# Hybrid encoder trunk: which tiles stand in a layer's opening, and where block 0's squares are summed

## The chip, the cores and the metric

The kernel runs on one core of a Trainium2 chip. The metric is device time in microseconds (us) of one execution; lower is better. The core has five engines with a queue each: TensorE (PE, matmuls, with its weight loads shown as PEld), VectorE (DVE), ScalarE (ACT), GpSimd (POOL) and SyncE (SP, which issues transfers). ACT issues transfers too; they are then named ACTq. Engines wait for each other by semaphores, and each engine works through its own instructions in order.

## The reference, cut to what matters

Two layers of an encoder over 2048 tokens of width 1024, float32. Each layer normalises the input, projects it by one wide matrix, and feeds the parts to a gated delta scan (branch A) and to a Conformer convolution (branch B):

```python
for l in range(2):
    h = rms_norm(x, norm_w[l])                        # mean of squares over 1024 channels
    proj = h @ w_in[l]                                # q,k,v | z_a | a,b | cf_val, cf_glu | z_b | gates
    q, k, v = silu(depthwise_conv(qkv, 5 taps))       # 4 heads of 128
    g, beta = f(a), sigmoid(b)                        # 16 scalar columns per token
    o = delta_forward(q, k, v, g, beta) + delta_backward(...)
    y_a = (rms_norm(o) * silu(z_a)) @ w_dn_out        # gate path of branch A
    u = silu(layer_norm(depthwise_conv(cf_val * sigmoid(cf_glu), 31 taps)))
    y_b = (u * silu(z_b)) @ w_cf_out                  # gate path of branch B
    x = x + (gate_a * y_a + gate_b * y_b) @ w_out
return rms_norm(x, final_norm_w)
```

## The kernel before, in words

Data lie channel-major: 8 tiles of 128 channels (`KD = 8`, index k) by 2048 tokens, the tokens in four blocks of 512 (`NB`). A normalised block `h` is kept as two parts, a high one and a low one (`split`, L156: ACT writes the high part by L157, DVE the low part by L158). Each weight tile of 128 columns (`weight`, L160) is loaded by SP as `wraw` in two pieces and split likewise into `whi` and `wlo`. A dense tile takes, for each k, three 128x512 matmuls: `whi` with `xhi` (L174), `whi` with `xlo` (L175), `wlo` with `xhi` (L176). One column tile on one block is thus 24 matmuls.

A layer runs through these stages: the opening (norm and first column tiles, block by block), four heads (convolved q, k and v tiles, the Conformer tile, then two gate-path tiles, `act_tile`, with columns 24 + j into `zb` and 12 + j into `za`), the first half of the merge-gate tiles (`gates(0)`), the delta scan, and the merge.

**The opening of layer 0.** The generator `first_norm` (L287) normalises the four blocks, and the code that makes column tiles pulls it on by `need` and `step_lead`. For a block: x is loaded by SP in 8 tiles, ACT squares them (L308), the squares are added up, ones times the sum (`token_sum`, four 128x1 matmuls, L200) gives the sum over channels for each token, DVE makes the reciprocal root (from `nv`, L316, to `nr`), `spread` (L206, L208) puts it on all partitions, DVE multiplies x by it (L327), and `split` makes `h`. Block 0 adds its squares on DVE, blocks 1 to 3 on POOL (L310). Block 3 loads its x twice: once into the buffers of the squares, since the tiles for x are still in use, and later for the product.

On TensorE a block of the opening has 64 matmuls: 16 of the scalar tile (`scalar_tiles`, L398; high and low part of the 16 scalar columns stand in one weight tile `wab`; L408, L409) and 24 each of the k and q tiles of head 0 (columns 4 and 0). The scalar tile's sum is copied out by ACT to `ab` (L411) and transposed by TensorE (L414) into one PSUM tile for all blocks. The k and q sums go to `cin` (L529); after each half of the tokens DVE convolves them (L553).

**Buffers.** The staging pool `st` has three buffers of 128x512 for the whole kernel: squares (`sqa`, `sq`), the diagonal matrices of `spread` (`dg`), `ab`, the gate-path outputs (`ao`) and others. Dense sums take three PSUM tiles (`pd`), the rest five (`pz`).

**What sets the order.** Instructions are given to the engines in the order of a schedule that is made when the program is built, from the written order and from the buffers; the excerpts below show it. Beside this there is a planner by hand: `post` and `back` hold generators of pieces of later work (keys, values, Conformer norms), and each `dense` pumps them on by a credit (`rate`, in us per tile: 3.0, 3.7 and 4.5 for convolved tiles, others of the heads, and gates). After `gates(0)`, filler steps run while `back` isn't empty (`while self.back` in `layer`). The filler is `gates(1)` and then `early_merge`, whose matmuls read `uop`. The delta scan (`delta`) pulls the rest of the filler between its own steps by a written plan. At its end, the last chunk's output is squared on ACT (L1022), scaled (L1040), transposed (L1045), multiplied by the gate path (L1046), stored and read back as `gop`, whose matmuls begin the merge.

## Time and profile before

| What | Value |
|---|---|
| median of 3 runs (range) | 3219.36 us (3217.04 to 3219.66) |
| the profiled execution | 3223.96 us, its span 3222.2 us |
| granted TensorE clock, mean of the span | 0.987 |
| TensorE busy | 3101.0 us (96%) |
| VectorE, ScalarE, GpSimd busy | 2401.9 us (75%), 1393.5 us (43%), 302.2 us (9%) |
| opening of layer 0: first dense matmul, first matmul of block 3 | 22.26 us, 96.26 us |

In the rows of the timeline there stand the start in us from the span's start, the duration in us, the engine, the line, the operation, output<-input, the count, and in brackets how long the engine had been idle and what released it. A row of waits reads: engine, its tile and line, what it waited for, the total in us, how often, the longest. A dense matmul's duration (0.38 us at the full clock) is longer than its share of the engine, since matmuls overlap: starts are 0.21 to 0.22 us apart, at half clock 0.42 to 0.43. A 128x1 sum of four columns shows as eight matmuls.

### The profile page before, as it was taken

How to read it: one execution, taken by the hardware profiler on the slowest of the kernel's cores; microseconds unless marked ns; L12 is line 12 of the kernel's file. 1: busy time of each engine (PE TensorE's matmuls, PEld its weight loads, DVE VectorE, ACT ScalarE, POOL GpSimd, SP SyncE). 2: the span in 40 equal slices, each digit the busy share in tenths (PEclk: the TensorE clock that was granted, in tenths of full speed). 3: DMA queues.
4: the chain of work that ended last, by engine and by line, in shares of the span. 5: the costliest groups of instructions: out<-in, count | busy, mean ns of one | idle time of the engine just before them, and what ended most of it. 6: DMA issues, size and time to landing. Idle time of an engine off the chain costs nothing. (4 is left out here: it accounts for less than half of the span.)

```text
span 3222.2 us, 51090 instructions
## 1 busy us (share of the span) xinstructions
PE 3101.0 (96%) x19110; PEld 2711.5 (84%) x19110; DVE 2401.9 (75%) x4409; ACT 1393.5 (43%) x3104; POOL 302.2 (9%) x297
## 2 busy tenths in 40 slices
PE   6999999999999999799999999999999999989997
PEld 5788888888889998687888888888888999877786
DVE  7789898987555687645666989898955567867655
ACT  5625252522344466533345242425234445655332
POOL 3000000000022231000000000000002122200000
PEclk9999999999999999899999999999999999999999
DMA  4233232334687785654413131314358777856644
GB/s 139 88 96 94 84 100 78 102 108 132 215 289 231 261 270 174 191 187 128 141 50 107 66 116 62 119 59 122 116 188 269 236 254 246 265 155 208 206 128 147
DMA packets 427030, 501.67 MB, mean 156 GB/s; under 512 B 95712, under 2 KB 260192, under 8 KB 426784
## 3 DMA queue, kind: packets, MB, share of 16 engines
q1 hardware_dynamic: 354032, 388.58, 38.9%
q10 hardware_dynamic: 64688, 80.09, 7.1%
q0 software_dynamic: 8064, 29.76, 2.4%
q8 instruction: 150, 2.46, 0.3%
q14 instruction: 96, 0.79, 0.1%
HBM read 342.74 MB, written 155.58 MB: 155 GB/s over the span
## 5 line engine op out<-in xcount | busy, mean ns | idle before, releaser
L174 PE MATMUL pd<-h,whi 128*128 128x512 f32 x2816 | 1091.7, 388 | 0.0
L176 PE MATMUL pd<-h,wlo 128*128 128x512 f32 x2816 | 1071.3, 380 | 2.3 <-DVE wlo L158 2.3
L175 PE MATMUL pd<-h,whi 128*128 128x512 f32 x2816 | 1072.1, 381 | 0.0
L728 DVE SCALAR_TENSOR_TENSOR cacc<-gp,vec,cacc 128x1009 f32<-128x1009 f32 (+1 forms) x480 | 615.5, 1282 | 37.8 <-ACT cacc L726 34.7
L174 PEld LDWEIGHTS pd<-h,whi 128*128 128x128 f32 x2816 | 534.6, 190 | 79.3 <-issue 1.4
L176 PEld LDWEIGHTS pd<-h,wlo 128*128 128x128 f32 x2816 | 534.4, 190 | 79.5 <-DVE wlo L158 3.9
L175 PEld LDWEIGHTS pd<-h,whi 128*128 128x128 f32 x2816 | 534.5, 190 | 72.9 <-issue 1.9
L157 ACT ACTIVATE whi<-wraw 128x512 fp32r<-128x512 f32 x400 | 243.0, 624 | 488.6 <-PE pd L175 346.6
L158 DVE TENSOR_TENSOR wlo<-wraw,whi 128x512 fp32r<-128x512 f32 x400 | 279.7, 713 | 175.8 <-ACT whi L157 163.9
L553 DVE SCALAR_TENSOR_TENSOR acc<-cin,vec,acc 128x1022 f32<-128x1022 f32 (+1 forms) x192 | 246.9, 1300 | 14.7 <-ACT acc L551 13.6
L176 PE MATMUL pd<-yhi,wlo 128*128 128x512 f32 x512 | 195.3, 381 | 8.0 <-DVE wlo L158 7.9
L174 PE MATMUL pd<-yhi,whi 128*128 128x512 f32 x512 | 194.7, 380 | 1.4 <-ACT whi L157 1.3
L175 PE MATMUL pd<-ylo,whi 128*128 128x512 f32 x512 | 194.0, 379 | 0.0
L808 ACT ACTIVATE go<-pd,vec 128x512 f32<-128x512 f32 x128 | 87.0, 680 | 133.2 <-PE pd L176 122.6
L529 ACT ACTIVATE cin<-pd 128x512 f32<-128x512 f32 x96 | 57.0, 593 | 156.3 <-PE pd L176 156.1
L174 PE MATMUL pd<-gop,whi 128*128 128x512 f32 x256 | 99.9, 392 | 20.5 <-ACT gop L157 19.3
L176 PEld LDWEIGHTS pd<-yhi,wlo 128*128 128x128 f32 x512 | 96.7, 189 | 25.6 <-DVE wlo L158 12.2
L174 PE MATMUL pd<-uop,whi 128*128 128x512 f32 x256 | 102.9, 402 | 12.8 <-ACT uop L157 7.1
L1210 ACT ACTIVATE gt<-gt 128x1024 f32<-128x1024 f32 x64 | 67.6, 1058 | 108.1 <-DMA gt<-gt 98.9
L740 ACT ACTIVATE ao<-pd 128x512 f32<-128x512 f32 x64 | 38.3, 598 | 170.0 <-PE pd L176 169.9
L976 ACT ACTIVATE dm<-pz,eg 128x128 f32<-128x128 f32 x240 | 68.5, 368 | 98.8 <-PE pz L970 93.7
L174 PEld LDWEIGHTS pd<-yhi,whi 128*128 128x128 f32 x512 | 96.8, 189 | 16.4 <-ACT whi L157 3.0
(296 smaller groups left out, 4837.0 us busy)
## 6 DMA issues: line engine op xcount, KB each, us to landing
wraw<-w_in SPq DMA_DIRECT2D x240, 256.0 KB, 3.2
gt<-go ACTq DMA_DIRECT2D x128, 256.0 KB, 3.4
dl<-gr SPq DMA_DIRECT2D x128, 256.0 KB, 5.1
dl<-kq SPq DMA_DIRECT2D x64, 512.0 KB, 5.9
dl<-kv SPq DMA_DIRECT2D x64, 512.0 KB, 5.2
gt<-gt SPq DMA_DIRECT2D x64, 512.0 KB, 5.0
wraw<-w_out SPq DMA_DIRECT2D x96, 256.0 KB, 3.0
kq<-acc SPq DMA_DIRECT2D x16, 1024.0 KB, 5.5
```

The costliest lines, as they stand in the source:

```text
L157: self.nc.scalar.activation(hi, src, AF.Copy)
L158: self.nc.vector.tensor_tensor(out=lo, in0=src, in1=hi.bitcast(F32), op=ALU.subtract)
L174: mm(ps, whi[:, k, :], xhi, start=k == 0, stop=False)
L175: mm(ps, whi[:, k, :], xlo, start=False, stop=False)
L176: mm(ps, wlo[:, k, :], xhi, start=False, stop=k == kk - 1)
L529: nc.scalar.activation(cut(t[:, o + b * NB:o + (b + 1) * NB]), sort(ps), AF.Copy)
L553: self.nc.vector.scalar_tensor_tensor(out=out, in0=t[:, k:k + n], scalar=wc(k), in1=out, op0=ALU.mult, op1=ALU.add)
L728: self.nc.vector.scalar_tensor_tensor(out=acc, in0=t[:, k:k + n], scalar=wc(k), in1=acc, op0=ALU.mult, op1=ALU.add)
L740: nc.scalar.activation(cut(o), sort(ps), func)
L808: nc.scalar.activation(cut(o), sort(ps), AF.Identity, bias=self.vec[:, V_GB + j:V_GB + j + 1])
L976: nc.scalar.activation(hv(o1)[:, hd, :], pq[:, hd, :], AF.Copy, scale=eg[:, hd:hd + 1])
L1210: nc.scalar.activation(gt, gt, AF.Sigmoid)
```

## The change

The opening of each layer takes other tiles. `opening` runs, for each block, the scalar tile and the two gate-path tiles of head 0 (`zb` column 24 and `za` column 12) k by k: two scalar matmuls, three of `zb`, three of `za`, then the next k; in block 3 they run one tile after the other. The transposes of a block's scalar tile (`turned`) are written at k = 3 of the next block. The convolved k and q tiles of head 0 follow after the opening over all four blocks, as those of the other heads do. The gate paths of heads 1 to 3 are made after the Conformer tiles of the head ahead of them; after the last head no gate path follows. The sum of gate paths, convolved tiles and scalar tiles is the same as before. The gate tiles of head 0 no longer pump the planner's credit. Block 0's squares aren't added on DVE: for each k four 128x1 matmuls (`token_add`, L205 in the changed file) add the square into the same four PSUM columns. The lines of the changed file are shifted: L308 is L314 there, L408/L409 are L422/L423, L411 is L445, L414 is L429, L208 is L213, the opening's gate outputs are written by L449, L1022 is L1046, L1040 is L1064, L1045 is L1069, L1163 is L1187.

```diff
--- before.py
+++ after.py
@@ -199,6 +199,11 @@
         for i in range(n):
             self.nc.tensor.matmul(ps[:, i:i + 1], src[:, i * P:(i + 1) * P], self.ones[:, 0:1],
                                   start=True, stop=True)
+
+    def token_add(self, ps, src, n, first, last):
+        for i in range(n):
+            self.nc.tensor.matmul(ps[:, i:i + 1], src[:, i * P:(i + 1) * P], self.ones[:, 0:1],
+                                  start=first and i == 0, stop=last, skip_group_check=True)
 
     def spread(self, ps, r, n):
         dg = self.pst.tile([P, NB], F32, tag="st", name="dg").rearrange("p (a b) -> p a b", b=P)
@@ -299,18 +304,21 @@
             if blk < 3:
                 for k in range(KD):
                     self.load(x[k], src[k])
-            acc = self.st("sqa")
-            eng = nc.gpsimd if blk else nc.vector
+            acc = None if blk == 0 else self.st("sqa")
+            ps = self.pz()
+            eng = nc.gpsimd
             for k in range(KD):
-                sq = self.st("sq0") if k else acc
+                sq = self.st("sq0") if k or not blk else acc
                 if blk == 3:
                     self.load(sq, src[k])
                 nc.scalar.activation(sq, sq if blk == 3 else x[k], AF.Square)
-                if k:
+                if not blk:
+                    self.token_add(ps, sq, 4, k == 0, k == KD - 1)
+                elif k:
                     eng.tensor_tensor(out=acc, in0=acc, in1=sq, op=ALU.add)
             yield
-            ps = self.pz()
-            self.token_sum(ps, acc, 4)
+            if blk:
+                self.token_sum(ps, acc, 4)
             v = self.sm(4, "nv")
             r = self.sm(4, "nr")
             nc.vector.tensor_scalar(out=v, in0=ps[:, 0:4], scalar1=1.0 / D, scalar2=EPS,
@@ -361,11 +369,13 @@
         self.gt_d = self.drm.tile([16, P, L], F32, name=f"gt{l}")
         self.o_d = self.drm.tile([NCH, P, H, P], F32, name=f"o{l}")
         self.og_d = self.drm.tile([H, P, L], F32, name=f"og{l}")
+        pt = self.opening()
         for j in range(H):
-            self.head(j)
+            self.head(j, pt)
             self.conformer(j)
-            self.act_tile(24 + j, self.zb_d[j], AF.Silu)
-            self.act_tile(12 + j, self.za_d[j], AF.Silu)
+            if j + 1 < H:
+                for col, dst in self.gate_paths(j + 1):
+                    self.act_tile(col, dst, AF.Silu)
         for blk in range(4):
             self.back.append(self.conformer_norm(blk))
         self.rate = R3
@@ -395,25 +405,51 @@
         nc.scalar.activation(w[:, :, 32:128], self.ones[:, None, 0:96].to_broadcast([P, KD, 96]), AF.Copy, scale=0.0)
         self.wab = w
 
-    def scalar_tiles(self):
+    def gate_paths(self, j):
+        return (24 + j, self.zb_d[j]), (12 + j, self.za_d[j])
+
+    def opening(self):
         nc = self.nc
-        w = self.wab
+        mm = nc.tensor.matmul
         pt = self.pz()
-
-        def block(blk):
-            xs = self.hx(blk)
-            ps = self.pd()
+        cols = self.gate_paths(0)
+        ws = [self.weight(self.a["w_in"][self.l, c], KD) for c, _ in cols]
+        turn = deque()
+
+        def scalar_steps(ps, xs):
             for k in range(KD):
                 xhi, xlo = (mix(x) for x in xs(k))
-                nc.tensor.matmul(ps, w[:, k, :], xhi, start=k == 0, stop=False)
-                nc.tensor.matmul(ps, w[:, k, :], xlo, start=False, stop=k == KD - 1)
-            ab = self.st("ab")
-            nc.scalar.activation(cut(ab[0:32, :]), sort(ps[0:32, :]), AF.Copy)
+                mm(ps, self.wab[:, k, :], xhi, start=k == 0, stop=False)
+                mm(ps, self.wab[:, k, :], xlo, start=False, stop=k == KD - 1)
+                yield
+
+        def turned(blk, ab):
             for i in range(4):
                 c = 4 * blk + i
                 nc.tensor.transpose(pt[:, c * 32:(c + 1) * 32], ab[0:32, i * P:(i + 1) * P], self.ident[0:32, 0:32])
 
-        return block, pt
+        for blk in range(4):
+            self.need(blk)
+            xs = self.hx(blk)
+            pss = [self.pd() for _ in range(3)]
+            runs = [scalar_steps(pss[0], xs)] + [self.dense_steps(ps, w, xs, KD) for ps, w in zip(pss[1:], ws)]
+            for group in [runs] if blk < 3 else [[r] for r in runs]:
+                for k in range(KD):
+                    for r in group:
+                        next(r)
+                    if k == 3 and turn:
+                        turned(*turn.popleft())
+                    if k % (2 if blk < 3 else 4) == 0:
+                        self.step_lead(2 if k == 0 else 1)
+            ab = self.st("ab")
+            nc.scalar.activation(cut(ab[0:32, :]), sort(pss[0][0:32, :]), AF.Copy)
+            turn.append((blk, ab))
+            for ps, (_, dst) in zip(pss[1:], cols):
+                o = self.st("ao")
+                nc.scalar.activation(cut(o), sort(ps), AF.Silu)
+                self.astore(dst[:, blk * NB:(blk + 1) * NB], o)
+        turned(*turn.popleft())
+        return pt
 
     def scalars(self, pt):
         nc, l, a = self.nc, self.l, self.a
@@ -503,7 +539,7 @@
         nc.vector.tensor_copy(t[:, 0:2 * pad], prev[:, HALF - pad:HALF + pad])
         return t, 2 * pad
 
-    def conv_tiles(self, cols, block=None):
+    def conv_tiles(self, cols):
         nc = self.nc
         self.rate = R1
         ws = [self.weight(self.a["w_in"][self.l, c], KD) for c in cols]
@@ -515,20 +551,13 @@
                 cur.append(self.padded(half, TAPS, prev[i], "cin") if half or not i else None)
             for b in range(2):
                 blk = 2 * half + b
-                self.need(blk)
-                if block:
-                    self.step_lead(2)
-                    block(blk)
                 for i, c in enumerate(cols):
-                    self.step_lead(2)
                     ps = self.pd()
                     self.dense(ps, ws[i], self.hx(blk), KD)
                     if cur[i] is None:
                         cur[i] = self.padded(half, TAPS, prev[i], "cin")
                     t, o = cur[i]
                     nc.scalar.activation(cut(t[:, o + b * NB:o + (b + 1) * NB]), sort(ps), AF.Copy)
-            if half == 0 and self.l:
-                self.need(2)
             for i, c in enumerate(cols):
                 t, o = cur[i]
                 prev[i] = t
@@ -563,15 +592,10 @@
             if q % 2:
                 yield
 
-    def head(self, hd):
-        nc = self.nc
-        v_ = nc.vector
+    def head(self, hd, pt):
         if hd == 0:
-            block, pt = self.scalar_tiles()
-            kt, qt = self.conv_tiles([4, 0], block)
             self.post.append(self.scalars(pt))
-        else:
-            kt, qt = self.conv_tiles([4 + hd, hd])
+        kt, qt = self.conv_tiles([4 + hd, hd])
         vs = self.pds.tile([P, 16], F32, tag="vs", bufs=2, name="vs")
         self.post.append(self.keys(hd, kt, qt, vs))
         vt, = self.conv_tiles([8 + hd])
```

Where the instructions stand now, at three places. ACT, from the end of block 0 of layer 0's opening: `ab` is the scalar tile's copy, `ao` are the gate outputs, `sqa` and `sq0` block 2's squares, `h1` is block 1. Before:

```order
L411 ACTIVATE ab_301<-pd_284 32x512
L529 ACTIVATE cin_174<-pd_329 128x512
L308 ACTIVATE sqa_407<-x0m_396 128x512
L308 ACTIVATE sq0_409<-x0m_396 128x512
L308 ACTIVATE sq0_412<-x0m_396 128x512
L308 ACTIVATE sq0_415<-x0m_396 128x512
L157 ACTIVATE h1_231<-x0_106 128x512 x2
L308 ACTIVATE sq0_418<-x0h_397 128x512
```

and of the change:

```order
L445 ACTIVATE ab_398<-pd_250 32x512
L157 ACTIVATE h1_261<-x0_106 128x512
L449 ACT_TABLE_LOAD
L449 ACTIVATE ao_400<-pd_251 128x512
L449 ACTIVATE ao_403<-pd_252 128x512
L151 DMA zb0_173<-ao_400 128x512
L157 ACTIVATE h1_261<-x0_106 128x512
L151 DMA za0_172<-ao_403 128x512
L157 ACTIVATE h1_261<-x0_106 128x512 x2
L314 ACTIVATE sqa_435<-x0m_424 128x512
L157 ACTIVATE h1_261<-x0_106 128x512
L314 ACTIVATE sq0_438<-x0m_424 128x512
```

Two evictions to staging buffers and their stores now stand ahead of block 2's squares. `sqa_435` is given the buffer of `ao_400` and `sq0_438` that of `ao_403`; `sq0_441` and all later squares of the block are given the buffer of `sq0_438`, as the third one belongs to `ab_398`.

TensorE, at the end of block 1: L200 is the sum of block 2's squares, L213 its spread, L429 the transposes of blocks 0 and 1. Before, the sum of block 2 stands in the middle of block 1 (`L408`, `L174` to `L176` with `h1`):

```order
L176 MATMUL pd_496<-h1_231,wlo_155 128x512
L200 MATMUL pz_430<-con_90,sqa_407 128x1 x4
L408 MATMUL pd_451<-h1_231,wab_101 128x512
L174 MATMUL pd_496<-h1_231,whi_154 128x512
L175 MATMUL pd_496<-h1_231,whi_154 128x512
```

and of the change:

```order
L174 MATMUL pd_413<-h1_261,whi_180 128x512
L200 MATMUL pz_436<-con_90,sqa_435 128x1 x4
L175 MATMUL pd_413<-h1_261,whi_180 128x512
L176 MATMUL pd_413<-h1_261,wlo_181 128x512
L174 MATMUL pd_414<-h1_261,whi_190 128x512
L175 MATMUL pd_414<-h1_261,whi_190 128x512
L176 MATMUL pd_414<-h1_261,wlo_191 128x512
L213 MATMUL pz_495<-dg_496,con_90 128x128 x4
L429 MATMUL pz_179<-con_90,ab_398 128x32 x4
L429 MATMUL pz_179<-con_90,ab_567 128x32 x4
```

Only five matmuls of block 1 are left behind the sum, and both blocks' transposes come after the spread.

ACT, at the end of layer 0's delta scan: `t` are evictions of the filler's `uop` tiles, `whi` weight splits, `junk,oss` the squares of the last chunk, `dm` its scales, `gop` the merge's operand. Before:

```order
L1022 ACTIVATE junk,oss<-dm_6984 128x128 x8
L157 ACTIVATE whi<-wraw 128x512
L1163 ACTIVATE t_10818<-pd 128x512
L157 ACTIVATE whi<-wraw 128x512
L1163 ACTIVATE t_10818<-pd 128x512 x2
L1040 ACTIVATE dm_6984<-dm_6984,orr 128x128 x8
L1163 ACTIVATE t_10818<-pd 128x512
L157 ACTIVATE whi<-wraw 128x512
L157 ACTIVATE gop<-gop 128x1024 x4
```

and of the change:

```order
L1046 ACTIVATE junk,oss<-dm_7053 128x128 x8
L1187 ACTIVATE t_10709<-pd 128x512
L157 ACTIVATE whi<-wraw 128x512
L1187 ACTIVATE t_10709<-pd 128x512
L1064 ACTIVATE dm_7053<-dm_7053,orr 128x128 x8
L157 ACTIVATE gop<-gop 128x1024 x4
```

Behind the last squares four evictions are now two and three weight splits one: TensorE has 12 `uop` matmuls between the last chunk's transposes and those before them, where it had 36, because one more filler tile runs ahead of the scan. Layer 1 has the same.

## The prediction

> **What bounds the kernel now.** The page comes first, then the windows of the first 250 us (busy us of each engine), then the waits of TensorE there.
>
> ```profile
> PE 3101.0 (96%) x19110; PEld 2711.5 (84%) x19110; DVE 2401.9 (75%) x4409; ACT 1393.5 (43%) x3104; POOL 302.2 (9%) x297
> ```
> ```profile
> 0.00:50.00 50.00, 29.13 (x105) 22.76 (x105) 31.54 (x68) 25.76 (x43) 16.85 (x17) 0.93 0.48 167
> 50.00:100.00 50.00, 39.47 (x172) 31.39 (x173) 43.52 (x80) 25.89 (x40) 15.02 (x10) 0.90 0.29 84
> 100.00:150.00 50.00, 48.67 (x247) 42.36 (x246) 38.24 (x73) 35.47 (x73) 1.27 (x2) 1.00 0.32 93
> 150.00:250.00 100.00, 100.00 (x504) 88.64 (x503) 78.71 (x153) 31.52 (x72) 6.99 (x10) 1.00 0.29 93
> ```
> ```profile
> ...
> PE pz L200 <- POOL sqa L310: 4.0, 3, 2.4
> PE pz L414 <- ACT ab L411: 2.5, 1, 2.5
> ```
>
> TensorE is busy 3101.0 of 3222.2 us. Of the 121 us that it idles, 50 − 29.13 + 50 − 39.47 = 31.4 lie in the first 100, and none from 150 to 250. From about 100 us on, then, every us by which TensorE starts later is a us at the end. The change keeps TensorE's work per block of the opening (16 scalar and 48 dense matmuls), so I ask one thing: when does block 3, the last, start on TensorE? These are TensorE's first matmuls of blocks 0, 1 and 3.
>
> ```profile
> 22.26 0.80 PE L408 MATMUL pd<-h,wab 128*128 128x512 f32 x1 [1.50 <-ACT h L157]
> 47.35 0.38 PE L408 MATMUL pd<-h,wab 128*128 128x512 f32 x1
> 96.26 0.80 PE L408 MATMUL pd<-h,wab 128*128 128x512 f32 x1 [1.50 <-ACT h L157]
> ```
>
> I call the end of block 0 on TensorE P (47.35 before). In the sum the anchor is 96.26: stalls ahead of it are in it already.
>
> **Block 0, squares summed in PSUM.** Seven adds on DVE go, seven more groups of four 128x1 matmuls come. Such a group, and what follows the sum now:
>
> ```profile
> 13.64 1.87 PE L200 MATMUL pz<-con,sqa 128*128 128x1 f32 x8 [13.64 <-DMA x<-x]
> 54.76 1.08 PE L200 MATMUL pz<-con,sqa 128*128 128x1 f32 x8 [2.39 <-POOL sqa L310]
> 19.60 0.68 DVE L158 TENSOR_TENSOR wlo<-wraw,whi 128x512 fp32r<-128x512 f32 x1
> ```
>
> A group takes 1.87 us at the start's slow clock and 1.08 at the full one. The adds kept up with the loads; slow groups do not: eight of them from about 6 us, each started some 1.7 us after the last, end near 20 instead of 15.5, +4.5. At the full clock they would end near 16, +0.5. Two weight splits of 0.68, now behind the sum on DVE, cost up to 1 more. So P moves by +1.5 to +5, to between 48.9 and 52.4; I take the upper half, since the row at 13.64 is the nearer one.
>
> **Block 2's squares.** Here the change adds its main wait. The staging pool has three buffers, for scalar tile, gate outputs and squares alike. Before, at the end of block 0 only the scalar tile took one, and its transposes freed it at once. Now block 0's scalar tile holds one until its transposes, which stand behind block 1 on TensorE (the second excerpt of the order); the gate outputs zb and za hold the other two until their stores have landed. Block 2's sqa waits for the zb store, its first sq0 for the za store, and each later square for the add on POOL that reads the square before it, since only that buffer is left. Squares, adds and stores now:
>
> ```profile
> 42.70 0.62 ACT L308 ACTIVATE sqa<-x0m 128x512 f32<-128x512 f32 x1
> 43.98 10.73 POOL L310 TENSOR_TENSOR sqa<-sqa,sq 128x512 f32<-128x512 f32 x7 [12.64 <-ACT sq L308]
> L310 POOL TENSOR_TENSOR sqa<-sqa,sq x21: 1272/1592/1726, 18.1 to 85.0; 128x512 f32<-128x512 f32 x21
> L151 ACTq DMA_DIRECT2D za<-ao x32: 326/326/327, 216.4 to 2288.5; - x32
> L740 ACT ACTIVATE ao<-pd x64: 577/605/607, 195.0 to 2287.9; 128x512 f32<-128x512 f32 x64
> DMA to landing us min/median/max: 2.0/2.2/7.0
> ```
>
> Before, these ran ahead of P: first square at 42.70, adds back to back, done at 54.71, that is P + 7.4. Now: two evictions of 0.605, an issue of 0.33, the zb store landed after 2.2, so the first square at about P + 4. The za store is an issue later; with its square of 0.62 and an add of 1.59 the first add ends at P + 7. Six more rounds of square 0.62, add 1.59 and a handoff of 0.1, 2.3 each, end at P + 21. With two buffers the square would hide behind the add. From the sum to the products x, then to TensorE, the rows of block 3 give:
>
> ```profile
> 90.26 0.16 DVE L316 TENSOR_SCALAR nv<-pz 128x4 f32<-128x4 f32 x1
> 94.79 2.06 DVE L327 SCALAR_TENSOR_TENSOR x0m<-x0m,vec,pz 128x512 f32<-128x512 f32 x3 [1.35 <-PE pz L208]
> 65.34 2.07 DVE L327 SCALAR_TENSOR_TENSOR x0m<-x0m,vec,pz 128x512 f32<-128x512 f32 x3 [3.88 <-PE pz L208]
> ```
>
> 4.53 from nv to x and 6.0 from nv to TensorE (90.26 to 96.26). With 1.87 for the group of sums, block 2's x starts at P + 21 + 1.9 + 4.5 = P + 27.3. Before it was 65.34 = P + 18.0. Queued behind the waiting squares on ACT are block 1's own splits and the evictions of block 1; behind the sum of block 2 on TensorE, block 1's last five matmuls.
>
> **Block 3's squares.** Their loads on SP use the same buffers: the second and third wait for the stores of block 1's gate outputs, whose evictions wait for those five matmuls and for the spread of block 2, near P + 27. With 0.605, the issue, 2.2 and a little queueing the second load issues near P + 31. How long loads, squares and adds then take, by block 3 before (first sq load, last add, and one of two conv starts on ACT that no longer stand between):
>
> ```profile
> 63.65 8.41 SPq L145 DMA_DIRECT2D sq<-x  x4
> 85.03 1.64 POOL L310 TENSOR_TENSOR sqa<-sqa,sq 128x512 f32<-128x512 f32 x1 [1.76 <-ACT sq L308]
> 71.96 1.14 ACT L551 ACTIVATE acc<-cin,vec 128x1022 f32<-128x1022 f32 x1
> ```
>
> 86.67 − 63.65 = 23.0, less 2 × 1.14 at best: 20.7 to 23.0. The sums end near P + 52.3 to P + 54.6; 1.9 and 6.0 more, with handoffs 8.2, put block 3 on TensorE at P + 60.5 to P + 62.8. With P from 48.9 to 52.4 that is 109.4 to 115.2 against 96.26: +13 to +19. I take **+16**. The convs leave this stretch of DVE; DVE no longer sets its end, so this is worth nothing here. The gate tiles moved forward are TensorE work taken from later, 0.
>
> **Layer 1's opening.** Before, transposes waited for the eviction, and slow matmuls followed:
>
> ```profile
> 1630.88 0.43 PE L414 MATMUL pz<-con,ab 32*128 32x32 f32 x4 [1.73 <-ACT ab L411]
> 1632.66 0.63 PE L175 MATMUL pd<-h,whi 128*128 128x512 f32 x1
> 1633.08 0.63 PE L176 MATMUL pd<-h,wlo 128*128 128x512 f32 x1
> 1636.27 0.38 PE L175 MATMUL pd<-h,whi 128*128 128x512 f32 x1
> 1636.48 0.38 PE L176 MATMUL pd<-h,wlo 128*128 128x512 f32 x1
> ```
>
> Deferred transposes remove 1.73, and perhaps the eight slow matmuls (starts 0.42 apart instead of 0.21): 1.7 more. The spreads there now share the three buffers with stored gate outputs: 1.4 back, bounded by 0 and by 2 × 2.2. **−2**, from −3.4 to +1.
>
> **The end of each delta scan.** Head by head, pumped work moves; one filler tile now goes ahead of the scan, so 12 instead of 36 uop matmuls stand in front of the last transposes. Before, in layer 0 and layer 1:
>
> ```profile
> 1297.38 2.45 ACT L1040 ACTIVATE dm<-dm,orr 128x128 f32<-128x128 f32 x8 [0.90 <-DVE orr L1036]
> 1298.27 1.94 PE L1045 MATMUL pz<-con,dm 128*128 128x128 f32 x8
> 1310.09 1.22 PE L174 MATMUL pd<-gop,whi 128*128 128x512 f32 x2 [9.88 <-ACT gop L157]
> 2883.30 1.22 PE L174 MATMUL pd<-gop,whi 128*128 128x512 f32 x2 [9.45 <-ACT gop L157]
> ```
>
> TensorE then idles 9.9 and 9.5 us for gop. The end of the chain is set by latency: squares of the last chunk on ACT, the root on DVE, the scales (1297.38), the transposes (1298.27), then stores and the load of gop. The uop matmuls beside it cover it. 24 fewer, 0.215 apart at the full clock (the last two rows of layer 1 above), are 5.2 us of cover gone, if the chain keeps its length; with two weight splits fewer ahead of it on ACT and DVE, it may come forward with the matmuls. 0 to 5.2 each, half: **+5** for both. The same matmuls done ahead of the scan are no extra work.
>
> Sum: 16 − 2 + 5 = +19. The profiled execution took 3223.96, 1.8 outside the span; 3224.0 + 19 = 3243 on its scale. The median of the runs shown, 3219.36, is 4.6 lower: **3238**.
>
> **Rivals.** *The clock comes up in block 0.* If the added groups count as work for the clock, they take 1.08 and P moves by 1.5 only: +13 − 2 + 5, 3235.
>
> ```profile
> 31.40 1.56 PE L200 MATMUL pz<-con,sqa 128*128 128x1 f32 x8 [1.37 <-POOL sqa L310]
> 38.51 0.42 PE L176 MATMUL pd<-h,wlo 128*128 128x512 f32 x1
> ```
>
> Against it: after a group at 31.40 the matmuls stayed slow to 38.51. The Trainium skill, "TensorE: Matmul & The Clock Gate", "What's actually happening", says that TensorE comes to its full clock after about 3.4 us of sustained work; by that rule the eight groups would warm it by themselves and the sum would be this rival's. The row at 31.40 speaks against counting so short a matmul, but it is one group, not eight.
>
> *The tails and the stores cost all*: 16 + 1 + 10.4, 3247.
>
> *Faster: DVE, not the buffers, sets block 3.* Before, block 3's sum was done at 86.73 + 1.05 = 87.78, but DVE read it at 90.26, 2.5 us later, since convs stood ahead (rows below). If the squares are still ready in time, this, the 2.5 of L414 and layer 1's 3.4 go, with free tails: 2.5 + 2.5 + 3.4 = 8.4 less, 3211. It decides if block 2's adds still end by P + 10. For it: POOL is only 4.0 us among TensorE's waits. Against: the adds ended at 54.71 and nv ran at 57.10, so 2.4 us is all the slack there is, and 13 are asked.
>
> ```profile
> 86.73 1.05 PE L200 MATMUL pz<-con,sqa 128*128 128x1 f32 x8 [0.21 <-POOL sqa L310]
> 78.66 10.29 DVE L553 SCALAR_TENSOR_TENSOR acc<-cin,vec,acc 128x1022 f32<-128x1022 f32 x6
> ```
>
> *Nothing in sum.* The ring costs only the first store wait, about 4, and layer 1 gives 3.4 back with free tails: 3220. This is also what is left if the wait is real but block 3's squares, loaded from their own transfers, catch up.
>
> **How the numbers follow.** Forecast 0.50, warm clock 0.13, full tails 0.14, faster 0.12, nothing in sum 0.11. The forecast's own terms reach from 13 − 3.4 + 0 = +9.6 to 19 + 1 + 10.4 = +30, 3229 to 3250. The range 3221 to 3250 leaves out the faster case and the edge of the last one, about 0.2. With 0.2%, 6.4 us, as what a measurement can tell from no change, slower is 0.50 + 0.13 + 0.14 = 0.77, the same 0.11, faster 0.12.
>
> **What would show it.** Right: POOL's adds of block 2 start between 54 and 58, about 2.3 apart rather than 1.5; TensorE's sum of block 2 waits some 10 us for POOL; TensorE's first matmul of block 3 lies at 109 to 115; layer 1's transposes show no wait; the waits for gop are longer than 9.9 and 9.5. Wrong: block 2's adds still ahead of P + 10, or block 3 on TensorE before 100, which would make the first term vanish; block 0's sums ending near 16 would show the warm clock; gop's waits unchanged would strike the +5.

## The result, and the profile after

The changed kernel takes 3300.66 us (3298.40 to 3310.14) against 3218.20 of the kernel before on the same chip: a ratio of 1.0262, 95% interval 1.0241 to 1.0284. That is 82 us slower. The forecast was 3238, +19, with a range that ended at 3250. The sign was right and the size was not. The ratios below leave out one execution, of the run called e11, which took twice as long as its eleven others.

The profiled execution took 3301.87 us, its span 3300.1 (before: 3223.96 and 3222.2). First the engines' busy time, then the windows of the first 250 us, columns as before.

```profile
PE 3140.5 (95%) x19166; PEld 2741.1 (83%) x19166; DVE 2370.5 (72%) x4402; ACT 1397.0 (42%) x3105; POOL 294.9 (9%) x297
```
```profile
0.00:50.00 50.00, 35.34 (x148) 31.34 (x149) 24.79 (x56) 20.00 (x33) 11.51 (x13) 0.97 0.60 209
50.00:100.00 50.00, 38.40 (x157) 31.71 (x156) 23.76 (x48) 22.07 (x38) 16.53 (x13) 0.82 0.22 64
100.00:150.00 50.00, 43.61 (x191) 37.16 (x192) 29.37 (x81) 19.97 (x33) 2.53 (x3) 0.84 0.14 45
150.00:250.00 100.00, 100.00 (x520) 88.89 (x519) 57.74 (x90) 51.76 (x117) 5.89 (x8) 1.00 0.31 91
```

TensorE's idle time is 3300.1 − 3140.5 = 159.6 us, where it was 121.2: +38.4. Its busy time grew by 39.5. Some 12 of these are block 0's 56 added matmuls (13.81 us below, instead of 1.87), in time that was idle before; the rest is matmuls that ran longer, at the slow clock: its mean over the span is 0.978, where it was 0.987. The windows show this at the opening: from 50 to 100 us the granted clock is 0.82 and was 0.90, from 100 to 150 it is 0.84 and was 1.00. So the new stops there are paid twice, as a wait and as slow matmuls behind it. The waits of TensorE over the whole span (microseconds in all, times, longest):

```profile
PE pz L590 <- ACT acc L569: 24.1, 6, 4.7
...
PE pd L174 <- ACT gop L157: 17.1, 2, 8.6
PE pz L200 <- POOL sqa L318: 12.4, 3, 5.5
...
PE pz L1069 <- ACT dm L1064: 6.6, 2, 3.6
PE pz L200 <- DVE lnt L790: 6.5, 4, 2.3
```

The top line is not at any place that the prediction priced. L590 holds the transposes of the convolved keys, six of them with a wait: heads 1, 2 and 3 of both layers. Before, the same waits (L561 there) were small:

```profile
PE pd L174 <- ACT gop L157: 19.3, 2, 9.9
...
PE pz L561 <- ACT acc L540: 8.8, 6, 1.6
```

Where the 78 us between the two spans arise can be counted. Both kernels give TensorE the same number of dense matmuls, 5824 in a layer. I take them in their order, and ask how much later the changed kernel starts the same one than the kernel before. An opening is counted as done at the 736th of its layer: there both kernels have gone through the same tiles. The heads end with the 2752nd, the scan with the 4480th. The column "e1" is the first experiment below.

| up to here | predicted for this part | lag of the changed kernel | lag of e1 |
|---|---|---|---|
| layer 0, opening done | +16 | +14.5 | +12.1 |
| heads done | 0 | +28.8 | +12.1 |
| delta scan done | +2.5 | +46.3 | +24.4 |
| merge done | 0 | +43.1 | +21.8 |
| layer 1, opening done | −2 | +44.3 | +22.0 |
| heads done | 0 | +59.4 | +21.2 |
| delta scan done | +2.5 | +78.9 | +36.0 |
| end | 0 | +78.2 | +35.7 |

The first opening's term came out close. The heads, priced at nothing, cost 14.3 and 15.1. The stretch from the gates to the scan's end, priced at 2.5 each, cost 17.5 and 19.5. Part of that lies at the gates themselves: in layer 0 the waits there for VectorE's pieces of the Conformer norm (`lnt`, the sums over channels, and `dg`, its spread) are 11.9 us, where they were 3.5.

**The opening.** TensorE's sums of the squares of blocks 0 and 2, and its first matmul of block 3:

```profile
5.36 13.81 PE L205 MATMUL pz<-con,sq 128*128 128x1 f32 x64 [5.36 <-ACT sq L314]
...
70.96 1.86 PE L200 MATMUL pz<-con,sqa 128*128 128x1 f32 x8 [5.49 <-POOL sqa L318]
...
109.92 0.80 PE L422 MATMUL pd<-h,wab 128*128 128x512 f32 x1 [0.94 <-ACT h L157]
```

Block 3 starts at 109.92 instead of 96.26, +13.7. ACT at the end of block 0, and POOL's adds of block 2, first, second and last:

```profile
50.07 0.57 ACT L445 ACTIVATE ab<-pd 32x512 f32<-32x512 f32 x1
...
51.17 1.28 ACT L449 ACT_TABLE_LOAD   x1
52.47 1.08 ACT L449 ACTIVATE ao<-pd 128x512 f32<-128x512 f32 x2
...
55.67 0.64 ACT L314 ACTIVATE sqa<-x0m 128x512 f32<-128x512 f32 x1 [0.25 <-DMA zb<-ao]
```
```profile
57.57 1.28 POOL L318 TENSOR_TENSOR sqa<-sqa,sq 128x512 f32<-128x512 f32 x1 [21.08 <-ACT sq L314]
59.59 1.28 POOL L318 TENSOR_TENSOR sqa<-sqa,sq 128x512 f32<-128x512 f32 x1 [0.74 <-ACT sq L314]
...
69.65 1.26 POOL L318 TENSOR_TENSOR sqa<-sqa,sq 128x512 f32<-128x512 f32 x1 [0.74 <-ACT sq L314]
```

Six adds follow the first, each 2.0 us after the last: 1.28 of add and 0.74 of waiting for the next square, which has one buffer. But the first square waited for the store only 0.25 us. What had kept it until 55.67 were the rows ahead of it on ACT.

**The heads.** DVE, at the end of the second half of head 1's k convolution. L582 are the taps of that convolution (`acc`), L716 to L721 the steps of the triangular solve that head 0's keys need (`sol`), L720 and L721 its last two; L752, further below, are the taps of head 0's Conformer convolution (`cacc`), whose rows are 1009 wide in the first half of the tokens and 1039 in the second:

```profile
335.31 1.27 DVE L582 SCALAR_TENSOR_TENSOR acc<-cin,vec,acc 128x1026 f32<-128x1026 f32 x1
336.51 1.21 DVE L720 TENSOR_TENSOR sol<-sol,br 64x1024 f32<-64x1024 f32 x1
337.73 1.22 DVE L721 TENSOR_TENSOR sol<-sol,br 64x1024 f32<-64x1024 f32 x1
338.98 2.49 DVE L582 SCALAR_TENSOR_TENSOR acc<-cin,vec,acc 128x1026 f32<-128x1026 f32 x2
```

The convolution's result passes ACT (L569) and goes to TensorE (L590):

```profile
340.30 1.06 ACT L569 ACTIVATE acc<-acc 128x1026 f32<-128x1026 f32 x1 [4.18 <-DVE acc L582]
```
```profile
341.41 0.48 PE L590 MATMUL pz<-con,acc 128*128 128x128 f32 x1 [4.68 <-ACT acc L569]
```

Before, the solve had long ended when this convolution ran. DVE there has the last Conformer tap of the first half, the solve's last step, the first tap of the second half, and then the same convolution's taps (L553); TensorE waited 1.57 us:

```profile
223.96 1.26 DVE L728 SCALAR_TENSOR_TENSOR cacc<-gp,vec,cacc 128x1009 f32<-128x1009 f32 x1
...
245.19 1.22 DVE L697 TENSOR_TENSOR sol<-sol,br 64x1024 f32<-64x1024 f32 x1
...
256.36 1.29 DVE L728 SCALAR_TENSOR_TENSOR cacc<-gp,vec,cacc 128x1039 f32<-128x1039 f32 x1
...
277.51 4.88 DVE L553 SCALAR_TENSOR_TENSOR acc<-cin,vec,acc 128x1026 f32<-128x1026 f32 x4
```
```profile
254.85 1.24 ACT L726 ACTIVATE cacc<-gp,vec 128x1039 f32<-128x1039 f32 x1
```
```profile
282.34 0.33 PE L561 MATMUL pz<-con,acc 128*128 128x128 f32 x1 [1.57 <-ACT acc L540]
```

The row on ACT is the start of the Conformer convolution's second half. In the changed kernel that start, the solve's first step on DVE, and the Conformer taps where the first half ends and the second begins:

```profile
248.87 1.25 ACT L750 ACTIVATE cacc<-gp,vec 128x1039 f32<-128x1039 f32 x1 [12.04 <-DVE gp L741]
```
```profile
252.36 0.20 DVE L716 TENSOR_TENSOR solt<-sol 128x31 f32<-128x31 f32 x1
...
281.21 1.27 DVE L752 SCALAR_TENSOR_TENSOR cacc<-gp,vec,cacc 128x1009 f32<-128x1009 f32 x1
...
282.71 1.30 DVE L752 SCALAR_TENSOR_TENSOR cacc<-gp,vec,cacc 128x1039 f32<-128x1039 f32 x1
```

In both kernels the solve takes turns with the taps of the first half. Before, these were done at 225, and the solve then had DVE nearly to itself until 246; the second half started only behind it. Now the second half is set up on ACT at 249, as soon as its input is there (the row waits for `gp`). Its taps follow those of the first half without a gap, and tap and solve step go on taking turns. The solve lasts from 252 to 339 instead of from 203 to 246, twice as long, and its end falls into head 1's k convolution. TensorE waits 4.68 us for it instead of 1.57. The same is seen at 507 (3.68) and at 672 us (3.67), and three times in layer 1.

Slow matmuls follow the stop. The 5 us behind it, before and now, in the columns of the windows (the clock is the third number from the right):

```profile
282.00:287.00 5.00, 4.66 (x26) 4.19 (x27) 5.00 (x5) 3.94 (x15) 0.00 (x0) 1.00 0.77 214
```
```profile
341.00:346.00 5.00, 4.59 (x14) 3.82 (x15) 5.00 (x6) 2.96 (x13) 0.00 (x0) 0.66 0.99 302
```

A clock of 0.66 over 5 us is 5 × 0.34 = 1.7 us lost behind the stop. Layer 0's heads add up: three waits 12.0 − 4.4 = 7.6, three slow stretches 5.1, and 1.5 more of waits for `wlo`: 14.2, against the 14.3 of the table. The Trainium skill, "TensorE: Matmul & The Clock Gate", "What's actually happening", says that an idle window of some 3.4 us brings the clock down by half. The trace agrees in so far as the stop of 1.57 us leaves 1.00 and that of 4.68 is followed by 0.66. It doesn't agree with 3.4 us as the border: the stop of 1.73 us at layer 1's opening in the kernel before (1630.88, in the prediction) was followed by matmuls 0.42 apart as well.

### The profile page after: what moved, and what is told of

It reads as the page before. It is cut to its first block, busy times and chain, and to the rows that moved or that the text cites. A ratio compares the mean times of both kernels' runs of the same rounds, so it can differ in the third digit from the quotient of the medians.

```text
span 3300.1 us, 51190 instructions
## 1 busy us (share of the span) xinstructions
PE 3140.5 (95%) x19166; PEld 2741.1 (83%) x19166; DVE 2370.5 (72%) x4402; ACT 1397.0 (42%) x3105; POOL 294.9 (9%) x297
## 5 line engine op out<-in xcount | busy, mean ns | idle before, releaser
L174 PE MATMUL pd<-h,whi 128*128 128x512 f32 x2816 | 1100.1, 391 | 4.3 <-DVE xnh L1278 2.8
L176 PE MATMUL pd<-h,wlo 128*128 128x512 f32 x2816 | 1079.9, 383 | 4.3 <-DVE wlo L158 4.3
L752 DVE SCALAR_TENSOR_TENSOR cacc<-gp,vec,cacc 128x1009 f32<-128x1009 f32 (+1 forms) x480 | 614.5, 1280 | 50.8 <-ACT cacc L750 48.5
L174 PEld LDWEIGHTS pd<-h,whi 128*128 128x128 f32 x2816 | 539.0, 191 | 86.5 <-issue 4.7
L176 PEld LDWEIGHTS pd<-h,wlo 128*128 128x128 f32 x2816 | 538.4, 191 | 84.7 <-DVE wlo L158 7.0
L158 DVE TENSOR_TENSOR wlo<-wraw,whi 128x512 fp32r<-128x512 f32 x400 | 271.2, 690 | 146.5 <-ACT whi L157 145.4
L582 DVE SCALAR_TENSOR_TENSOR acc<-cin,vec,acc 128x1022 f32<-128x1022 f32 (+1 forms) x192 | 243.8, 1281 | 10.1 <-ACT acc L580 9.0
L176 PE MATMUL pd<-yhi,wlo 128*128 128x512 f32 x512 | 195.4, 382 | 5.8 <-DVE wlo L158 5.6
L174 PE MATMUL pd<-yhi,whi 128*128 128x512 f32 x512 | 194.8, 381 | 1.4 <-ACT whi L157 1.4
L174 PE MATMUL pd<-gop,whi 128*128 128x512 f32 x256 | 99.7, 391 | 18.2 <-ACT gop L157 17.1
L176 PEld LDWEIGHTS pd<-yhi,wlo 128*128 128x128 f32 x512 | 96.7, 189 | 23.7 <-DVE wlo L158 10.2
L174 PEld LDWEIGHTS pd<-yhi,whi 128*128 128x128 f32 x512 | 96.8, 189 | 16.8 <-ACT whi L157 3.6
L175 PEld LDWEIGHTS pd<-ylo,whi 128*128 128x128 f32 x512 | 96.8, 189 | 13.4
L174 PE MATMUL pd<-uop,whi 128*128 128x512 f32 x256 | 102.0, 398 | 4.3 <-ACT whi L157 4.2
L176 PE MATMUL pd<-gop,wlo 128*128 128x512 f32 x256 | 99.4, 388 | 6.9 <-DVE wlo L158 6.9
```

Source lines behind the costliest of these rows:

```text
L158: self.nc.vector.tensor_tensor(out=lo, in0=src, in1=hi.bitcast(F32), op=ALU.subtract)
L174: mm(ps, whi[:, k, :], xhi, start=k == 0, stop=False)
L175: mm(ps, whi[:, k, :], xlo, start=False, stop=False)
L176: mm(ps, wlo[:, k, :], xhi, start=False, stop=k == kk - 1)
L582: self.nc.vector.scalar_tensor_tensor(out=out, in0=t[:, k:k + n], scalar=wc(k), in1=out, op0=ALU.mult, op1=ALU.add)
L752: self.nc.vector.scalar_tensor_tensor(out=acc, in0=t[:, k:k + n], scalar=wc(k), in1=acc, op0=ALU.mult, op1=ALU.add)
```

## The experiments

All ratios are to the kernel before, run on the same chip. Two theories stood for the heads:

- **A, the planner's phase.** The change puts the entry that starts scalars, keys and solve (`post.append(self.scalars(pt))`) ahead of head 0's k and q tiles; before it stood behind them. Each dense tile (one column tile on one block) pulls the queue on by a piece. The scalars' pieces, which took up the first two tiles behind k and q, are then already done, so the keys and what follows them come two tiles earlier, and the theory takes this to last through the later heads.
- **B, DVE is too full.** Head 0's convolutions left the opening, where DVE had time, and now fill the heads; the waits come from the work, wherever the entry stands.

**e1, the entry behind head 0's k and q tiles again; e2, the kernel before with two extra pulls of the entry right behind it.** A says that e1 loses the waits and e2 gains them without any other part of the change; B says that e1 keeps them and e2 hardly moves.

```diff
 (e1, changed kernel)
     def head(self, hd, pt):
+        kt, qt = self.conv_tiles([4 + hd, hd])
         if hd == 0:
             self.post.append(self.scalars(pt))
-        kt, qt = self.conv_tiles([4 + hd, hd])
 (e2, kernel before)
             kt, qt = self.conv_tiles([4, 0], block)
             self.post.append(self.scalars(pt))
+            self.follow()
+            self.follow()
```

> The changed kernel, with head 0's scalar pieces queued behind its k and q tiles instead of ahead of them, as they were before. Nothing of the opening changes. Theory A (phase of the hand planner): the pieces queued two tiles earlier move keys, solve and the Conformer's second half forward by two tiles, the second half's taps then alternate with the solve on VectorE, the solve ends inside the next head's k convolution, and TensorE waits there. Then the six waits of the key transposes for acc (24.1 us in all now) fall to about 1.5 us each as before, and the 34 us lost between the openings and the gates of both layers (lag 14.5 to 30.5 and 43 to 61) go: about 3267 us. One more filler tile runs ahead of the scan, which may cost up to 10 us. Rival B (VectorE carries head 0's k and q convolutions later and never catches up): the waits stay at 3.7 to 4.7 us each, 3300 us.

> The kernel before, with two pulls of the scalar pieces right after they are queued, so that keys and solve come two tiles earlier; opening and everything else as before. Theory A: the waits for acc rise from 1.5 to about 4 us in each of six places and the time rises by about 34 us, to 3252 us, with no change in the opening. Rival B: 3218 us, since no convolution moves.

e1: 3261.27 us, 1.0130 [1.0115, 1.0145], 39 us less than the changed kernel. e2: 3261.63, 1.0134 [1.0114, 1.0153], 42 more than the kernel before, with the old opening. TensorE's waits, e1 first, then e2:

```profile
PE pz L1069 <- ACT dm L1064: 12.1, 2, 6.1
PE pz L590 <- ACT acc L569: 8.8, 6, 1.6
```
```profile
PE pz L561 <- ACT acc L540: 24.0, 6, 4.7
```

The waits leave with the entry's place and come with it, to the tenth: 8.8 and 24.0, against 8.8 before and 24.1 in the changed kernel. In e2 the Conformer convolution's second half also starts as soon as its input is there:

```profile
191.83 1.26 ACT L728 ACTIVATE cacc<-gp,vec 128x1039 f32<-128x1039 f32 x1 [12.05 <-DVE gp L719]
```

In e1 that row comes at 308.37, behind the solve's end at 299.6, as in the kernel before.

A is shown for the heads, in both directions, and B falls there. Of e1's lag the table says the rest: nothing in the heads, 12 in the opening, and still 10 and 14 from the end of the heads to the end of the layer.

**e3, gate outputs in buffers of their own; e8, block 0's squares added on DVE again.** Both undo one part of the opening. e3 takes the stores out of block 2's way, which was the prediction's main wait:

```diff
 (e3, changed kernel)
+        stage = self.mid("aom")
+        ring = Ring([stage[:, i * NB:(i + 1) * NB] for i in range(4)])
...
-                o = self.st("ao")
+                o = ring()
 (e8, changed kernel)
-            acc = None if blk == 0 else self.st("sqa")
+            acc = self.st("sqa")
...
-            eng = nc.gpsimd
+            eng = nc.gpsimd if blk else nc.vector
...
-                if not blk:
-                    self.token_add(ps, sq, 4, k == 0, k == KD - 1)
-                elif k:
+                if k:
                     eng.tensor_tensor(out=acc, in0=acc, in1=sq, op=ALU.add)
...
-            if blk:
-                self.token_sum(ps, acc, 4)
+            self.token_sum(ps, acc, 4)
```

> The changed kernel, with the gate-path outputs of the opening in a tile of the mid pool (four slots) instead of the three staging buffers. Theory of the staging buffers: block 2's adds on POOL no longer wait for the stores, the first starts near 45 us instead of some 60, and TensorE starts block 3 near 96 us instead of 109.9; the time falls by about 13 us, to 3287. Rival (the sums of block 0 on TensorE, or the loads, delay everything): block 3 starts no earlier than 105 us, 3297 or more.

> The changed kernel with block 0's squares added on VectorE as before, everything else changed. If the sums in PSUM delay block 0, nv comes at 15.5 instead of some 20 us, block 0 ends about 4 us earlier and the time falls by about 4 us, to 3297; if the loads or the later work hide it: 3300.

e3: 3302.95, 1.0262 [1.0245, 1.0279], as the changed kernel. POOL's first adds of block 2 there:

```profile
59.26 1.30 POOL L318 TENSOR_TENSOR sqa<-sqa,sq 128x512 f32<-128x512 f32 x1 [22.46 <-ACT sq L314]
61.29 1.28 POOL L318 TENSOR_TENSOR sqa<-sqa,sq 128x512 f32<-128x512 f32 x1 [0.74 <-ACT sq L314]
```

They start no sooner (59.26 against 57.57) and have the same 0.74 between them. The stores were not what they waited for. Block 3 starts at 107.54 instead of 109.92, a gain of 2.4 that the total doesn't show. e8: 3301.39, 1.0265 [1.0243, 1.0286]. In its trace block 3 starts on TensorE at 103.75 instead of 109.92, so the PSUM sums cost some 6 us in the opening; the total doesn't show it, its runs lie 15 us apart.

**e4, the gates pump more.** The gates' rate is 5.0 instead of 4.5 us of planned work for each tile, so that the filler tile that runs ahead of the scan (the prediction's tail term) isn't needed.

```diff
-R3 = 4.5
+R3 = 5.0
```

> The changed kernel, with the planner's credit per gate tile at 5.0 instead of 4.5, so that the queue is empty at the end of the first gate half and no filler tile runs ahead of the scan, as before. If the filler tile taken early is what lengthens the ends of the two scans (the waits of the last transposes for the scales, 6.6 us in all, new), these waits vanish and the time falls by about 10 us, to 3290. If the ends are bound by the chain of loads and stores alone, it stays at 3300.

3294.02, 1.0235 [1.0220, 1.0250], 6.6 less. Waits:

```profile
PE pz L590 <- ACT acc L569: 24.0, 6, 4.7
PE pd L174 <- ACT gop L157: 19.0, 2, 10.2
PE pz L200 <- DVE lnt L790: 10.9, 4, 3.8
```

The heads are untouched. The wait for `dm` (6.6) is gone, that for `gop` is back at 19.0, and layer 0's lag no longer grows in the scan (38.2 in it, 38.1 behind). That is the tail. Its size isn't shown apart, since the gates' own waits for `lnt` rise from 6.5 to 10.9: the 6.6 us are what is left of it.

**e5, both: e1 with a rate of 5.25; e6, e5 with all the opening's outputs apart; e7, e6 with block 2's squares further ahead.** If phase and tail added up, e5 would leave only the opening. e6 and e7 then take the opening apart: the buffers first, then the place of the squares on ACT.

```diff
 (e5, on e1)
-R3 = 4.5
+R3 = 5.25
 (e6, on e5)
-            ab = self.st("ab")
+            ab = ring()
...
-                o = self.st("ao")
+                o = ring()
 (e7, on e6)
-                        self.step_lead(2 if k == 0 else 1)
+                        self.step_lead(2 if k == 0 or k >= 4 else 1)
```

> The kernel with the scalar pieces late (e1), and 5.25 instead of 4.5 of planner credit per gate tile, so that the queue is empty at the end of the first gate half and no filler tile runs ahead of the scan (two did in e1). If filler tiles taken early cost time at the end of the scan, the two rises of about 12 us at the scans' ends go: 3261 - 24 = 3237 us, 12 us of it the opening and some 5 the gates. If they cost nothing: 3261.

> e5 with the gate-path outputs and the scalar tile's copies of the opening in a tile of the mid pool, so that all three staging buffers serve the squares. Order theory: ScalarE still has the evictions of block 0 ahead of block 2's squares, so these start at about 55 us as before, but run 1.5 instead of 2.0 us apart; block 3 starts on TensorE some 4 to 6 us earlier than 109.9, the time is 3232. Theory of the staging buffers alone: squares start near 45 us, block 3 near 96, 3223.

> e6 with the norm's pieces pulled sooner in each block (two instead of one at k = 4 and 6), which puts block 2's squares ahead of block 0's evictions on ScalarE. Order theory: first add of block 2 before 47 us, block 3 on TensorE at 96 us or earlier, 14 us less than e5: about 3222. If the opening is bound by something else (block 0's sums, the loads), block 3 stays near 105 and the time near 3232.

e5: 3267.63, 1.0156 [1.0140, 1.0171]: a miss, it is not faster than e1 but slower. TensorE's waits from 800 to 900 us, where the gates lie, in e5:

```profile
PE pz L784 <- DVE lnt L779: 5.6, 2, 4.9
PE pz L200 <- DVE lnt L790: 3.8, 1, 3.8
```

In e1 that stretch had 1.8 and 1.7 us of waits. Pumping faster asks DVE for the norm's sums sooner than it can give them. What the scan's end gains the gates have lost: in layer 0 e5's lag goes from 13.8 behind the heads to 25.5 behind the first half of the gates and 27.9 behind the scan, that of e1 from 12.1 to 9.3 and 24.4.

e6: 3269.69, 1.0158 [1.0140, 1.0176], not to be told from e5. e7: 3256.60, 1.0121 [1.0101, 1.0141], 11 less than e5. POOL's adds of block 2, e6 and then e7:

```profile
58.58 10.00 POOL L318 TENSOR_TENSOR sqa<-sqa,sq 128x512 f32<-128x512 f32 x7 [22.02 <-issue]
```
```profile
41.43 1.27 POOL L318 TENSOR_TENSOR sqa<-sqa,sq 128x512 f32<-128x512 f32 x1 [4.97 <-ACT sq L314]
48.81 9.40 POOL L318 TENSOR_TENSOR sqa<-sqa,sq 128x512 f32<-128x512 f32 x6 [6.11 <-ACT sq L314]
```

With free buffers the adds run without the 0.74 between them but start as late; block 3 starts at 108.34 instead of 110.91. With the squares ahead of the evictions they are done at 58.2, and the opening's lag is 0.2 us. So the opening's cost is the order on ACT for the most part, some 10 us, and the ring of three staging buffers for about 3. The order was changed with the buffers already free, not alone.

**e9, a gate pair behind the last head again; e10, the opening mended, the rest as e1.** e1's remaining lag grows behind the heads. In the kernel before, a pair of gate-path tiles follows each of the four Conformer tiles; now the first pair is made in the opening, and none follows the last. A theory for the rest: TensorE's 41 us of such a pair were the time in which DVE worked off the planner's queue ahead of the gates. e9 makes head 3's pair twice, 41.4 us of matmuls in each layer on top, with the same values stored again.

```diff
 (e9, on e1)
-                if j + 1 < H:
-                    for col, dst in self.gate_paths(j + 1):
-                        self.act_tile(col, dst, AF.Silu)
+                for col, dst in self.gate_paths(min(j + 1, 3)):
+                    self.act_tile(col, dst, AF.Silu)
 (e10, on e1: e6, e7 and e8 together, with the rate of 4.5)
```

> e1 with the last head's two gate-path tiles made a second time behind the last Conformer tile (the same values are stored again): 8 dense tiles, 41.4 us of TensorE work in each layer, more, in the place where the kernel before had a gate pair. If the absence of that pair is what the gates and the ends of the scans lose (25 us in e1, of the 37 left there), VectorE catches up under the new work and the planner's queue is empty in time: 3261 + 83 - 25 = 3319 us. If these losses have another cause: 3344 us.

> e1 with what e7 and e8 changed in the opening: outputs and scalar copies in their own tile, the norm's pieces pulled sooner, block 0's squares added on VectorE. The opening's 12 us of loss should turn into some 7 us of gain against the kernel before (e7: lag 0.2 us behind the opening; e8: 7 less): 3261 - 19 = 3242 us; the rest, gates and ends of scans, stays. If the two mends do not add up: 3249.

e9: 3317.32, 1.0307 [1.0292, 1.0322]: 83 us of added TensorE work make the kernel 56 us longer than e1, so 27 come back, close to the 25 that were forecast. Its waits:

```profile
PE pd L174 <- ACT gop L157: 18.9, 2, 10.2
...
PE pz L200 <- DVE lnt L789: 4.3, 4, 1.6
```

The wait for `dm` is gone, 12.1 in e1, those for `lnt` are halved from 8.7, and `gop` is back to what it was before. e10: 3247.30, 1.0089 [1.0075, 1.0103], 14 less than e1. Its opening is 6.3 us ahead of the kernel before, and it still ends 28.7 behind it. By the profiled spans (3242.9 and 3222.2) it loses 27 us behind its opening, and e1 some 23 behind its own: that loss is there whatever the opening does, and the pair brings it back. What in the pair does it, the time that it gives DVE or the eight more tiles that pump the planner, these runs don't part for certain. e5 speaks for the time: its 32 gate tiles in a layer pump 0.75 us more each, 24 us of planned work, nearly the 8 × 3.7 = 29.6 of the pair but without added matmuls, and it gained nothing. It does so later than the pair, though.

**e11, the kernel before with the deferred transposes alone; e12, with the norm steps one further ahead as well.** The one part of the change that the traces show as a gain, put alone into the kernel before: the scalar tile's transposes stand behind the block's k tile.

```diff
 (e11, kernel before)
-            for i in range(4):
-                c = 4 * blk + i
-                nc.tensor.transpose(pt[:, c * 32:(c + 1) * 32], ab[0:32, i * P:(i + 1) * P], self.ident[0:32, 0:32])
+            def turned():
+                for i in range(4):
+                    c = 4 * blk + i
+                    nc.tensor.transpose(pt[:, c * 32:(c + 1) * 32], ab[0:32, i * P:(i + 1) * P], self.ident[0:32, 0:32])
+            return turned
...
                     self.dense(ps, ws[i], self.hx(blk), KD)
+                    if block and i == 0:
+                        turned()
 (e12, on e11)
-                    self.step_lead(2)
+                    self.step_lead(3)
```

> The kernel before, with the scalar tile's transposes written behind the block's k tile instead of ahead of it; nothing else. If the waits of the transposes for the copy (2.5 and 1.7 us, with slow matmuls behind the second) are on the path: 6 us less, 3212. If the next wait (block 3's sum read late by VectorE) takes their place in layer 0: 3215. No effect: 3218.

> e11 with three instead of two pieces of the norm pulled at each place, so that VectorE reads block 2's and 3's sums ahead of part of the convolutions. If VectorE's order holds block 3 back in the kernel before: 2 to 4 us less than e11, 3209. If the squares' loads or POOL set it: as e11.

e11: 3213.42, 0.9978 [0.9968, 0.9989], 5 us faster than the kernel before and the fastest of all here. Layer 1's wait for `ab`, 1.73, is gone; in layer 0 one of 2.50 is left, at 78.17, and block 3 starts at 89.79 instead of 96.26. e12: 3222.44, 1.0011 [1.0003, 1.0020], a miss: it gives the gain back. Its sum of block 3 waits for POOL:

```profile
80.34 1.86 PE L200 MATMUL pz<-con,sqa 128*128 128x1 f32 x8 [4.64 <-POOL sqa L310]
```

In e11 that sum, at 82.18, shows no wait. Asked for sooner, TensorE stands before the squares instead of before its own matmuls.

## Why the prediction was wrong in size

Of the 82 us the runs put 39 on the planner's phase (the changed kernel less e1, and 42 by e2; some 30 of them in the heads, most of the rest at the gates). Of what e1 keeps, some 12 are layer 0's opening, and the others, 23 by the profiled spans and some 30 by the medians, lie behind the heads; the gate pair brings 27 back (e9).

- **Opening of layer 0, predicted +16: right in size, wrong in part of its cause.** Block 3 came at 109.92, inside 109.4 to 115.2; the lag was 14.5. Right: the slow groups of block 0 (their sum was read at 19.21, forecast near 20), block 1's first matmul at 50.92 (P, forecast 48.9 to 52.4), adds from 54 to 58 (57.57), one buffer for seven squares (2.0 apart, I said 2.3: an add takes 1.28 here and not 1.59). Wrong: "Block 2's sqa waits for the zb store". It waited 0.25 us. The squares are late because ACT has them behind the evictions, and k by k these come at the very end of the block: `ab` at 50.07, where before it came at 41.40; e3 and e6 against e7 settle it. That the first square still came at P + 4.8, near the forecast P + 4, is luck: the rows ahead of it on ACT, a table load of 1.28 among them, filled the time that was priced for the store. The sum also has a slip of 0.6: P + 31 and 20.7 to 23.0 are P + 51.7 to P + 54.0, not P + 52.3 to P + 54.6. The wait of TensorE there was 5.5 us rather than 10.
- **Warm clock, 0.13: refuted.** The 64 matmuls of 128x1 took 13.81 us, 1.73 a group, near the slow group's 1.87 and far from 1.05. By the rule of the Trainium skill ("TensorE: Matmul & The Clock Gate", "What's actually happening") that some 3.4 us of sustained work warm TensorE, the last groups would have been fast; here they were not, so the measurement decides. The row at 31.40 was a weak witness against it: its 1.56 lie between a fast group and a slow one, since the granted clock went from 1.00 to 0.51 inside it, at 31.7.
- **Heads, priced at 0: wrong, the largest part.** The step that failed is in the first part: "From about 100 us on, then, every us by which TensorE starts later is a us at the end", and with it the choice to price only the opening, layer 1's opening and the tails. The sum carried TensorE's delay through the heads and gave no price to what the new place of `post.append` does to DVE's order there. What the runs showed in its place: the solve's end falls into the next head's k convolution, TensorE waits 4.7, 3.7 and 3.7 us there in a layer, and with the slow matmuls behind the stops the heads cost 14.3 and 15.1. The windows from 150 to 250 were full before and are full now; the new stops come from 336 us on.
- **"The gate tiles moved forward are TensorE work taken from later, 0": wrong.** The sum of the work was right, but that pair stood where the gates needed it ahead of them; gone from there, some 27 us are lost (e9 brings them back, and e10 loses as much behind a mended opening).
- **Scan ends, predicted +5: near in size by the waits, wrong in form.** The wait for `gop` did not grow, as I had said, but fell from 19.3 to 17.1. The stop came one step earlier, at the transposes waiting for `dm` (6.6). Net +4.4; e4 takes it away and gains 6.6, gates included.
- **Layer 1's opening, predicted −2: wrong, by about 3.** The wait for `ab` went, as forecast, but the lag rose by 1.2, from 43.1 to 44.3, just outside the −3.4 to +1 that was given. Of the stored gate outputs I had feared 1.4; instead one matmul waits 2.8 us for `xnh`, a tile of the merge's result that DVE writes, and slow matmuls follow this stop as they followed the old one. Why DVE is later with it no run shows:

```profile
PE pd L174 <- DVE xnh L1278: 2.8, 1, 2.8
```

- **Rivals.** "Faster" asked for block 2's adds to end by P + 10, and "nothing in sum" for block 3 to catch up; the adds ended at 70.91, P + 20, and block 3 came at 109.92. "Full tails" was nearest by its time, by luck: the reason wasn't its own. No rival held that the planner would order DVE's work otherwise in the heads, and DVE's order there, unlike that of ACT and TensorE around the opening, was not weighed at all.

What stays open: why the Conformer convolution's second half is set up so early when the queue runs two tiles ahead. That it is, and that the solve then ends late, is read from the order of the rows in four runs (before, changed, e1, e2); no run changed its buffers alone. The changed opening with a gate pair left for the last head, without added work, was not tried. e8's and e6's gains of some 6 and 3 us are seen in their traces' openings alone.

## What to carry to other kernels

A planner that is pumped by credits has a phase, and an edit that moves one entry of its queue by two tiles moves work on engines and in stages that the diff doesn't touch: one such line cost 40 us here, nearly all of it more than 200 us behind the line's own place. Price every stage that the queue runs through, and read the order of the engine that is waited for, not only of the one that the edit names. Work that is moved forward leaves a gap in the cover at its old place. And a stop can cost more than its wait: behind each of the three new ones in layer 0's heads, 3.67 to 4.68 us long, some 1.7 us more went in slow matmuls.

## What the hardware showed that was not expected

TensorE stayed at its slow pace through 64 back-to-back matmuls of 128x1, 13.81 us long, 1.73 for eight, where eight took 1.05 in the kernel before at 86.73. The clock column reads 1.00 for that stretch, so at the start of a profile the durations are the better witness. A stop well below 3 us can also be followed by slow matmuls (1.73 us at 1630.88 before), and another of that length is not (1.57 at 282.34). And POOL's add of a 128x512 tile is not one price but two: of the seven of block 2 in e6, two took 1.60 us and five 1.26 to 1.28, all with the squares at hand. What sets it no run here shows. Behind each other they start 1.33 to 1.69 apart, against 2.0 with one buffer.
